# A two-layer decoder step: gemms that add onto PSUM banks seeded by ScalarE, and token sums of the embedding taken four tiles at a time

## The chip, the cores and the metric

One core of a Trainium2 chip runs the whole program. The metric is the device time of one execution in microseconds; the number given for a kernel is the median of its timed runs.

## What is computed

The reference is one inference step of a two-layer decoder on 576 tokens (512 of a prompt, 8 x 8 of samples), width 2048. Cut to what matters here:

```python
y = rmsnorm(x)
proj = y @ w_in                       # 2048 -> 6144: pool input, pool gate, q, k, v, retention gate
o = retention(rope(q), rope(k), v)    # 4 heads of 256
o = head_rmsnorm(o) * silu(gate)
p = pool_mixer(pool_in) * silu(gate)  # 4 groups, windows 2, 4, 8, 16
x2 = x + rmsnorm(concat(p, o) @ w_out)
e = rmsnorm(p_embed @ w_ple)          # per-layer embedding, 256 -> 2048
x = x2 + sigmoid(x2 @ w_gate + b) * e
```

The states of retention and pooling are updated and returned as well.

## The kernel before, in words

Everything is held transposed: 128 features on the partitions, 576 tokens along a row, in two halves of 288 columns (`HN`). A product in float32 precision is made of three float32r matmuls (high x high, high x low, low x high), so weights and activations are split into a high part (ScalarE, L90) and a low part (VectorE, L91).

Each layer has three phases. `in_first` multiplies the first half of the contraction of `w_in` in a Strassen-like scheme (`unit`, L234) and stores 48 tiles in DRAM (`proj_dram`). `in_phase` (L469) takes the second half: `columns(pr)` (L472) loads the stored tile into a buffer `part`, splits two weight blocks and calls `gemm` (L129): 48 matmuls of 288 columns into two PSUM banks `acc`. Then VectorE adds the banks onto the loaded tile (L484), and the consumer works on the tile in SBUF: `rotary` (L491, L492), the gates (L500), v (L579), the pool inputs (L669, L670). There are four `acc` banks, that is two pairs, four `part` buffers and two `g` buffers. Heads 0 to 3 come first (q, k, v, gate: eight tiles each), then pool groups 3, 2, 1, 0 (four tiles each).

`out_phase` multiplies by `w_out`, takes the norm (`rsqrt`, L294), and then makes the embedding: 16 tiles of 12 matmuls each (L767), whose squares (L316, ScalarE) are summed over the partitions by `token_sums` (L290, L292): for each tile four float32 matmuls of a matrix of ones, 144 tokens each, into four groups of 32 columns of TensorE. ScalarE also copies each bank to SBUF (L771). Then come the gates of the layer.

`rsqrt` is a chain that crosses engines: token sums on TensorE, twelve small steps on VectorE (L300 to L306), four matmuls that spread the row (L310, "picks"), two copies by ScalarE (L311). A head ends with it: its output, two tiles `o`, is squared (L635, L636), multiplied by the result (L640) and by the gate (L653), which is the last read of a `g` buffer. Ahead of the squares stand four transposes (L628) with two small adds (L632). The head's keys are transposed (L549) and scaled (L93 on ScalarE, L94 on VectorE). The states of the samples are updated four at a time (L376) between matmuls L359 and L375.

The order of the instructions on each engine is not written by hand: a scheduler sets it from its own estimates when the kernel is built. An engine runs its list strictly in that order, and a tile of a pool waits until the last reader of the buffer's previous tile is done.

Of the kernel before, what the change touches and what calls it, by code (L numbers as in the profile page):

```python
# [10 lines left out]
AF = mybir.ActivationFunctionType  # L11
ALU = mybir.AluOpType
# [21 lines left out]
def half(ap, h):  # L34
    return ap[:, h * HN:(h + 1) * HN]
# [3 lines left out]
def decoder_kernel(ctx: ExitStack, tc: tile.TileContext, a, decay8):  # L39
# [6 lines left out]
    def buf(tag, shape=(P, NT), dt=F32):  # L46
        return sb.tile(list(shape), dt, tag=tag, name=tag, bufs=BUFS.get(tag, 1))
# [75 lines left out]
    def mix_tile():  # L123
        return ps.tile([P, 512], F32, tag="po", name="po", bufs=2)
# [1 line left out]
    def bank(shape):  # L126
        return ps.tile(list(shape), F32, tag="pb", name="pb", bufs=2)

    def gemm(w, xs, new=acc_tile, by_half=False):  # L129
        acc = [new()[:, :HN] for _ in range(2)]  # L130
        n = len(w)
        for hs in ((0,), (1,)) if by_half else ((0, 1),):
            for i, ((wh, wl), (xh, xl)) in enumerate(zip(w, xs)):
                for passno, (u, v) in enumerate(((wh, xh), (wh, xl), (wl, xh))):
                    for h in hs:
                        nc.tensor.matmul(  # L136
                            acc[h], u, v[:, h * HN:(h + 1) * HN],
                            start=(i == 0 and passno == 0), stop=(i == n - 1 and passno == 2),
                        )
        return acc  # L140

# [148 lines left out]
    def token_sums(sums, src, start, stop):  # L290
        for q in range(4):
            nc.tensor.matmul(sums[32 * q:32 * q + 32], ones, src[:, q * QN:(q + 1) * QN], start=start, stop=stop)  # L292

    def rsqrt(out, srcs, n, sums=None):  # L294
        if sums is None:
            sums = mix_tile()[:, :QN]
            for i, src in enumerate(srcs):
                token_sums(sums, src, i == 0, i == len(srcs) - 1)
        v, t, r = (w[:, i * QN:(i + 1) * QN] for w in (tmp(),) for i in range(3))
        nc.vector.tensor_scalar(v, sums, 1.0 / n, EPS, op0=ALU.mult, op1=ALU.add)  # L300
        nc.vector.tensor_scalar(r.bitcast(I32), v.bitcast(I32), 1, None, op0=ALU.logical_shift_right)
        nc.vector.tensor_scalar(r.bitcast(I32), r.bitcast(I32), -1.0, float(0x5F3759DF), op0=ALU.mult, op1=ALU.add)
        for _ in range(3):
            nc.vector.scalar_tensor_tensor(out=t, in0=r, scalar=-0.5, in1=r, op0=ALU.mult, op1=ALU.mult)
            nc.vector.tensor_tensor(out=t, in0=t, in1=v, op=ALU.mult)
            nc.vector.scalar_tensor_tensor(out=r, in0=t, scalar=1.5, in1=r, op0=ALU.add, op1=ALU.mult)  # L306
        for h in range(2):
            rows = mix_tile()[:, :HN]
            for q in (2 * h, 2 * h + 1):
                nc.tensor.matmul(rows[:, (q % 2) * QN:(q % 2 + 1) * QN], pick[:, q], r, start=True, stop=True)  # L310
            nc.scalar.copy(half(out, h), rows)  # L311

    def square(out, src):
        if isinstance(src, list):
            for h in range(2):
                nc.scalar.activation(half(out, h), src[h], AF.Square)  # L316
        else:
            nc.scalar.activation(out, src, AF.Square)

# [11 lines left out]
    def load_tables():  # L331
# [6 lines left out]
        consts["kdec_s"] = load_const("kdec_s", [P, NH, NS])  # L338
        consts["mask_s"] = load_const("mask_s", [P, NH, 64])
        consts["invcnt"] = load_const("invcnt", [P, 4, 16])  # L340

    def after_all(ins, others):
        for other in others:
            tc.add_manual_dep(
                ins.ins, other.ins.name, mybir.DependencyInfo(mybir.DependencyClass.Sync, mybir.DependencyReason.DATA),
                reason="one burst",
            )

    def retention_state(l, h, s0_ring, qrep, kst, vst, po_s):
        for bg in range(2):  # L350
# [118 lines left out]
    def in_phase(l, raws, r2, rB, cos, sin):  # L469
        b_ring, st_ring, rot_ring, s0_ring = Ring(0, 12), Ring(12, 4), Ring(16, 8), Ring(24, 4)  # L470

        def columns(pr):  # L472
            keys = [("in2", p) for p in pairs] + [("out", 0, 0), ("out", 0, 1)]
            i = keys.index(("in2", pr))
            raw = raws.pop(("in2", pr))
            for c in range(2):
                t = buf("part")
                nc.sync.dma_start(out=t, in_=proj_dram[l][2 * pr + c])
                w = split_weights(raw, 8 * c, 8)
                if c == 1:  # L480
                    fetch(l, raws, keys[i + 1:i + 3])
                acc = gemm(w, r2)
                for h in range(2):
                    nc.vector.tensor_tensor(out=half(t, h), in0=acc[h], in1=half(t, h), op=ALU.add)  # L484
                yield t

        def rotary(pr):
            x = [rot_ring.tile() for _ in range(2)]
            u = [buf("d") for _ in range(2)]
            for i, t in enumerate(columns(pr)):  # L490
                nc.vector.tensor_tensor(out=x[i], in0=t, in1=cos, op=ALU.mult)  # L491
                nc.vector.tensor_tensor(out=u[i], in0=t, in1=sin, op=ALU.mult)  # L492
            nc.vector.tensor_tensor(out=x[0], in0=x[0], in1=u[1], op=ALU.subtract)
            nc.vector.tensor_tensor(out=x[1], in0=x[1], in1=u[0], op=ALU.add)
            return x

        def silu_gates(pr):
            for t in columns(pr):
                g = buf("g")
                nc.vector.tensor_tensor(out=g, in0=t, in1=rB, op=ALU.mult)  # L500
                nc.scalar.activation(g, g, AF.Silu)
                yield g

# [56 lines left out]
        def head(h):  # L560
# [14 lines left out]
            kst = sample_rows(sample_part(k, "kdec_s", h), (0, 2))  # L575

            v = [rot_ring.tile() for _ in range(2)]
            for i, t in enumerate(columns(16 + h)):
                nc.vector.tensor_tensor(out=v[i], in0=t, in1=rB, op=ALU.mult)  # L579
            vt = token_major(v)  # L580
            vc = buf("smp", (P, 2, 64))
            for e in range(2):
# [73 lines left out]
        def pool_group(g):  # L656
# [6 lines left out]
            wh, wl = buf("u", (P, 2, DK), F32R), buf("u", (P, 2, DK), F32R)  # L663
            split(wh, wl, wraw)
            xs = []
            for i, t in enumerate(columns(g)):
                e = buf("d", (P, BUF + NP))
                nc.vector.memset(e[:, :BUF], 0.0)
                nc.vector.tensor_tensor(out=e[:, BUF:], in0=t[:, :NP], in1=rB[:, :NP], op=ALU.mult)  # L669
                nc.vector.tensor_tensor(  # L670
                    out=es[:, i, :, BUF:], in0=t[:, NP:].rearrange("p (b s) -> p b s", s=NS),
                    in1=rB[:, NP:].rearrange("p (b s) -> p b s", s=NS), op=ALU.mult,
                )
                nc.scalar.copy(npool[:, i, 0], e[:, NP:NP + BUF])
                nc.scalar.copy(npool[:, i, 1:], es[:, i, :, NS:])
                s, ss, sh = e, es[:, i], 1
                while sh < w:
                    n = tmp()[:, :BUF + NP]
                    m = buf("es", (P, NB, SEG))
                    lo = 2 * sh - 1  # L680
                    nc.gpsimd.tensor_tensor(out=n[:, lo:], in0=s[:, lo:], in1=s[:, sh - 1:BUF + NP - sh], op=ALU.add)
                    nc.gpsimd.tensor_tensor(out=m[:, :, lo:], in0=ss[:, :, lo:], in1=ss[:, :, sh - 1:SEG - sh], op=ALU.add)  # L682
                    s, ss, sh = n, m, 2 * sh
                p = tmp()
                nc.vector.tensor_tensor(out=p[:, :16], in0=s[:, BUF:BUF + 16], in1=consts["invcnt"][:, g], op=ALU.mult)
# [38 lines left out]
    def out_phase(l, raws, ops_out):  # L724
# [30 lines left out]
        for k in range(2):  # L755
# [3 lines left out]
            split(hi, lo, t)  # L759
            pp.append((hi, lo))  # L760
        sums = mix_tile()[:, :QN]
        for c8 in range(2):
            raw = load_weights(a["w_ple"][l, :, c8 * 8:(c8 + 1) * 8].rearrange("p c k n -> p (c k) n"))
            w = split_weights(raw, 0, 16)
            for c in range(8):
                ct = c8 * 8 + c
                acc = gemm(w[2 * c:2 * c + 2], pp)  # L767
                t, sq = buf("part"), buf("u")
                square(sq, acc)
                for i in range(2):  # L770
                    nc.scalar.copy(half(t, i), acc[i])  # L771
                token_sums(sums, sq, ct == 0, ct == KT - 1)
                nc.sync.dma_start(out=ple_dram[l][ct], in_=t)

        def residual(first):
            def xs(k):
# [192 lines left out]
```

## Time and profile before

| | us |
|---|---|
| timed runs, median (lowest to highest of 3) | 2215.37 (2213.88 to 2215.63) |
| the profiled execution | 2217.77 |
| its span on the core | 2216.0 |
| TensorE (PE) busy | 2185.6 (99%) |
| VectorE (DVE) busy | 1733.7 (78%) |
| ScalarE (ACT) busy | 1057.0 (48%) |
| GpSimd (POOL) busy | 174.5 (8%) |

The span is the time from the first to the last instruction on the engines. Busy time counts work; matmuls are pipelined, so a busy TensorE is judged by the distance from one matmul's start to the next one's. "Idle before" in a row is the time for which the engine waited just before, with the work that released it.

### The profile page before, as it was taken

What the parts mean: (1) busy time and instruction counts of PE and PEld (TensorE: products, weight loads), DVE (VectorE), ACT (ScalarE), POOL (GpSimd) and SP (SyncE); (2) the same over time, 40 slices, a digit from 0 to 9 for tenths busy, and PEclk for the clock granted to TensorE, in tenths of its full rate; (3) what the DMA queues carried; (4) which work ended last, traced back from release to release, by engine and by line L of the source; (5) the groups of instructions that cost most, each with busy time, mean ns of one, the idle gap of its engine ahead of it and who ended that gap; (6) DMA issues with size and microseconds to landing.
All of it is one profiled execution on the core that took longest, in us unless ns stands there. A gap on an engine that the chain in (4) does not pass through costs nothing.

```text
span 2216.0 us, 42622 instructions
## 1 busy us (share of the span) xinstructions
PE 2185.6 (99%) x16692; PEld 2143.3 (97%) x16692; DVE 1733.7 (78%) x3146; ACT 1057.0 (48%) x2097; POOL 174.5 (8%) x145
## 2 busy tenths in 40 slices
PE   8999999999999999999999999999999999999998
PEld 8999999999999999899999999999999899998998
DVE  8788766667689998788977886666676899988865
ACT  5465433444334555655545554434443345566532
POOL 2000000000043110000020000000002411100000
PEclk9999999999999999999999999999999999999999
DMA  6455455546443333556644444455555443345554
GB/s 222 149 195 165 155 168 165 169 157 191 154 159 129 133 128 122 196 176 208 216 157 149 169 156 152 160 177 173 164 164 165 155 135 130 106 149 192 176 194 156
DMA packets 137706, 361.99 MB, mean 163 GB/s; under 512 B 14496, under 2 KB 51872, under 8 KB 116640
## 3 DMA queue, kind: packets, MB, share of 16 engines
q1 hardware_dynamic: 137504, 359.26, 49.1%
q8 instruction: 131, 2.15, 0.4%
q14 instruction: 71, 0.58, 0.1%
HBM read 273.17 MB, written 86.04 MB: 162 GB/s over the span
## 4 chain that ended last, share of the span: by engine, by line
PE 87%; DVE 7%; DMA 4%; issue 2%; ACT 0%; SPq 0%; POOL 0%; DVEq 0%; ACTq 0%
PE acc L136 30%; PE acc L118 13%; PE acc L116 13%; PE acc L117 13%; PE acc L226 4%; PE pb L117 3%; PE pb L116 3%; PE pb L118 3%; DMA x<-ple 2%; DVE wl L91 1%; PE po L292 1%; PE po L359 1%; PE pb L375 1%; PE po L136 1%; PE pb L549 1%
## 5 line engine op out<-in xcount | busy, mean ns | idle before, releaser
L136 PE MATMUL acc<-m,wh 128*128 128x288 f32 x3584 | 661.1, 298 | 11.0 <-DVE part L484 11.0
L90 ACT CAST wh<-raw 128x512 fp32r<-128x512 f32 x567 | 350.5, 619 | 506.2 <-PE acc L136 260.7
L117 PE MATMUL acc<-m,wh 128*128 128x288 f32 x1944 | 572.8, 296 | 0.0
L116 PE MATMUL acc<-m,wh 128*128 128x288 f32 x1944 | 571.2, 295 | 0.5 <-ACT m L249 0.5
L118 PE MATMUL acc<-m,wl 128*128 128x288 f32 x1944 | 566.7, 295 | 0.7 <-DVE wl L91 0.7
L136 PEld LDWEIGHTS acc<-m,wh 128*128 128x128 f32 x3584 | 537.9, 190 | 19.1 <-issue 18.0
L91 DVE TENSOR_TENSOR wl<-raw,wh 128x512 fp32r<-128x512 f32 x567 | 407.2, 719 | 134.8 <-ACT wh L90 124.9
L136 PE MATMUL acc<-m,wl 128*128 128x288 f32 x1792 | 399.2, 296 | 0.0
L116 PEld LDWEIGHTS acc<-m,wh 128*128 128x128 f32 x1944 | 364.6, 188 | 1.9 <-ACT m L249 1.0
L117 PEld LDWEIGHTS acc<-m,wh 128*128 128x128 f32 x1944 | 364.9, 188 | 0.0
L118 PEld LDWEIGHTS acc<-m,wl 128*128 128x128 f32 x1944 | 362.4, 188 | 1.4 <-DVE wl L91 1.4
L90 ACT CAST wh<-S 128x512 fp32r<-128x512 f32 x356 | 220.4, 620 | 252.9 <-PE acc L117 139.7
L136 PEld LDWEIGHTS acc<-m,wl 128*128 128x128 f32 x1792 | 294.6, 190 | 1.9 <-issue 1.3
L91 DVE TENSOR_TENSOR wl<-S,wh 128x512 fp32r<-128x512 f32 x356 | 250.5, 705 | 22.0 <-ACT wh L90 20.5
L484 DVE TENSOR_TENSOR part<-acc,part 128x288 f32<-128x288 f32 x192 | 79.3, 449 | 62.4 <-PE acc L136 57.5
L239 POOL TENSOR_TENSOR S<-raw 128x512 f32<-128x512 f32 x45 | 70.3, 1562 | 713.6 <-DVE wl L91 352.6
L239 DVE TENSOR_TENSOR S<-raw 128x512 f32<-128x512 f32 x133 | 93.3, 701 | 8.5 <-DMA raw<-in_w_in 7.0
L682 POOL TENSOR_TENSOR es<-u 128x176 f32<-128x176 f32 x16 | 14.9, 937 | 1055.5 <-DVE u L670 1053.7
L117 PE MATMUL pb<-m,wh 128*128 128x288 f32 x324 | 95.5, 295 | 0.0
L116 PE MATMUL pb<-m,wh 128*128 128x288 f32 x324 | 95.1, 294 | 0.0
L118 PE MATMUL pb<-m,wl 128*128 128x288 f32 x324 | 95.1, 293 | 0.0
L249 ACT COPY d<-acc 128x288 f32<-128x288 f32 x228 | 86.1, 394 | 0.0
(265 smaller groups left out, 3412.1 us busy)
## 6 DMA issues: line engine op xcount, KB each, us to landing
raw<-in_w_in SPq DMA_DIRECT2D x95, 1024.0 KB, 5.3
raw<-in_w_out SPq DMA_DIRECT2D x32, 1024.0 KB, 4.9
raw<-in_w_gate SPq DMA_DIRECT2D x32, 1024.0 KB, 5.3
proj<-d SPq DMA_DIRECT2D x96, 288.0 KB, 2.1
part<-proj SPq DMA_DIRECT2D x96, 288.0 KB, 3.0
m<-in_state_ret SPq DMA_DIRECT2D x64, 256.0 KB, 3.1
out_new_ret_s<-m SPq DMA_DIRECT2D x64, 256.0 KB, 3.4
x<-m SPq DMA_DIRECT2D x48, 288.0 KB, 3.1
```

The costliest lines, as they stand in the source:

```text
L90: nc.scalar.copy(hi, src)
L91: return nc.vector.tensor_tensor(out=lo, in0=src, in1=hi.bitcast(F32), op=ALU.subtract)
L116: nc.tensor.matmul(out, wh, xh, start=start, stop=False, **kw)
L117: nc.tensor.matmul(out, wh, xl, start=False, stop=False, **kw)
L118: nc.tensor.matmul(out, wl, xh, start=False, stop=stop, **kw)
L136: nc.tensor.matmul(acc[h], u, v[:, h * HN:(h + 1) * HN], start=(i == 0 and passno == 0), stop=(i == n - 1 and passno == 2),)
L226: nc.tensor.matmul(acc[h], w[:, j], xs[h][passno == 1], start=(i == 0 and j == 0 and passno == 0), stop=(i == 1 and j == 3 and passno == 2),)
L239: eng.tensor_tensor(out=s, in0=x, in1=y, op=op)
L249: ops["tail_act"] = nc.scalar.copy(dst, src)
L292: nc.tensor.matmul(sums[32 * q:32 * q + 32], ones, src[:, q * QN:(q + 1) * QN], start=start, stop=stop)
L359: mm = nc.tensor.matmul(po_s[32 * r:32 * r + 32, bg], qrep[:, dt, b * 32:b * 32 + 32], s0s[r][:, dt], start=(dt == 0), stop=(dt == 1),)
L484: nc.vector.tensor_tensor(out=half(t, h), in0=acc[h], in1=half(t, h), op=ALU.add)
```

## The change

The loaded tile is no longer added behind the gemm. ScalarE copies it into the two banks first (the seed), the first matmul of each bank then adds instead of overwriting, and `columns` hands out the banks. So the consumers read PSUM, in two halves of 288 columns: rotary reads each bank twice, the gates and v once, the pool inputs in three pieces. In the embedding the squares go into other buffers, and `together` sums four tiles behind each other, with a dependency that makes the first of its matmuls wait for the last square.

```diff
-    def gemm(w, xs, new=acc_tile, by_half=False):
+    def gemm(w, xs, new=acc_tile, by_half=False, seed=None):
         acc = [new()[:, :HN] for _ in range(2)]
+        if seed is not None:
+            for h in range(2):
+                nc.scalar.copy(acc[h], half(seed, h))
...
-                            start=(i == 0 and passno == 0), stop=(i == n - 1 and passno == 2),
+                            start=(seed is None and i == 0 and passno == 0), stop=(i == n - 1 and passno == 2),
+                            skip_group_check=seed is not None,
...
+    def together(sums, srcs, start, stop):
+        for i, src in enumerate(srcs):
+            for q in range(4):
+                mm = nc.tensor.matmul(
+                    sums[32 * q:32 * q + 32], ones, src[:, q * QN:(q + 1) * QN],
+                    start=start and i == 0, stop=stop and i == len(srcs) - 1,
+                )
+                if q == i == 0:
+                    after_all(mm, [last_square[0]])
...
-                acc = gemm(w, r2)
-                for h in range(2):
-                    nc.vector.tensor_tensor(out=half(t, h), in0=acc[h], in1=half(t, h), op=ALU.add)
-                yield t
+                yield gemm(w, r2, seed=t)
+
+        def times(out, acc, row):
+            for h in range(2):
+                nc.vector.tensor_tensor(out=half(out, h), in0=acc[h], in1=half(row, h), op=ALU.mult)
...
-            for i, t in enumerate(columns(pr)):
-                nc.vector.tensor_tensor(out=x[i], in0=t, in1=cos, op=ALU.mult)
-                nc.vector.tensor_tensor(out=u[i], in0=t, in1=sin, op=ALU.mult)
+            for i, acc in enumerate(columns(pr)):
+                times(x[i], acc, cos)
+                times(u[i], acc, sin)
...
-                nc.vector.tensor_tensor(out=g, in0=t, in1=rB, op=ALU.mult)
+                times(g, acc, rB)
...
-                nc.vector.tensor_tensor(out=v[i], in0=t, in1=rB, op=ALU.mult)
+                times(v[i], acc, rB)
...
-                nc.vector.tensor_tensor(out=e[:, BUF:], in0=t[:, :NP], in1=rB[:, :NP], op=ALU.mult)
+                nc.vector.tensor_tensor(out=e[:, BUF:BUF + HN], in0=acc[0], in1=rB[:, :HN], op=ALU.mult)
+                nc.vector.tensor_tensor(out=e[:, BUF + HN:], in0=acc[1][:, :NP - HN], in1=rB[:, HN:NP], op=ALU.mult)
...
-                t, sq = buf("part"), buf("u")
+                t, sq = buf("part"), buf(("tmp", "tmp", "tmp", "tmp", "g", "g", "u", "u")[ct % 8])
...
-                token_sums(sums, sq, ct == 0, ct == KT - 1)
+                squares.append(sq)
+                if len(squares) == 4:
+                    together(sums, squares, ct == 3, ct == KT - 1)
+                    squares = []
```

The scheduler then places everything anew. The lines of the changed kernel stand some numbers further down: its gemm matmul is L141 (before L136), the seed L136, the transposes L647 (L628) and L568 (L549), token sums L298 (L292) and in the embedding L303, picks L326 (L310) and their copies L327 (L311), L659 and L672 are the products with the row and with the gate (L640, L653), and L504 is `times`.

The first place is TensorE at the end of head 0, where the transposes L628 stand. Before, they lie between the matmuls of the next gemm:

```order
L136 MATMUL acc<-m_2419,wh 128x288 x2
L628 MATMUL pb<-c_ident,u 128x128 x4
L136 MATMUL acc<-m_2420,wh 128x288 x2
L136 MATMUL acc<-m_2419,wl 128x288 x2
L136 MATMUL acc<-m_2569,wh 128x288 x2
L136 MATMUL acc<-m_2570,wh 128x288
L549 MATMUL pb<-c_ident,m_3972 128x128
L549 MATMUL pb<-c_ident,m_3973 128x128
```

With the change, in full names, they stand behind each other, and the next gemm comes only after the token sums:

```order
L141 MATMUL acc_4958<-m42_2719,wl_4952 128x288
L647 MATMUL pb_4488<-c_ident_969,u_4486 128x128 x4
L568 MATMUL pb_4532<-c_ident_969,m18_3976 128x128
L568 MATMUL pb_4532<-c_ident_969,m19_3977 128x128
...
L568 MATMUL pb_4543<-c_ident_969,m18_3976 128x128
L568 MATMUL pb_4543<-c_ident_969,m19_3977 128x128
...
L298 MATMUL po_4500<-tmp_4495,ones_61 32x144 x4
L298 MATMUL po_4500<-tmp_4496,ones_61 32x144 x4
L141 MATMUL acc_5050<-m28_1669,wh_5042 128x288
```

No gemm matmul is left among them. acc_5050 takes the bank of acc_4889 (the first tile of the keys); its seed waits for VectorE's last read of that bank, which stands there with the change:

```order
L651 TENSOR_TENSOR m23_4388<-m23_4388,pb_4488 128x64
L94 SCALAR_TENSOR_TENSOR m1_4538<-pb_4532,c_kdec_971,m0_4537 128x256
L504 TENSOR_TENSOR m18_4875<-acc_4889,long_2886 128x288
L504 TENSOR_TENSOR m18_4875<-acc_4890,long_2886 128x288
L504 TENSOR_TENSOR d_4877<-acc_4889,long_2887 128x288
L504 TENSOR_TENSOR d_4877<-acc_4890,long_2887 128x288
```

The reads of acc_4889 come behind L651 and L94, which work on what those transposes give.

The second place is VectorE at the end of head 3, where the pool groups begin, behind the last picks of the heads. Before (o is m22 and m23, part_7858 the loaded tile of the first gemm of pool group 2):

```order
L484 TENSOR_TENSOR part_7858<-acc_7870,part_7858 128x288
L640 TENSOR_TENSOR m22_7038<-m22_7038,tmp_7150 128x576
L640 TENSOR_TENSOR m23_7039<-m23_7039,tmp_7150 128x576
L484 TENSOR_TENSOR part_7858<-acc_7871,part_7858 128x288
L91 TENSOR_TENSOR wl_8155<-raw_7868,wh_8154 128x512
L653 TENSOR_TENSOR m22_7038<-m22_7038,g_7295 128x576
L653 TENSOR_TENSOR m23_7039<-m23_7039,g_7364 128x576
```

And with the change:

```order
L659 TENSOR_TENSOR m22_7084<-m22_7084,tmp_7196 128x576
L659 TENSOR_TENSOR m23_7085<-m23_7085,tmp_7196 128x576
L672 TENSOR_TENSOR m22_7084<-m22_7084,g_7341 128x576
L91 TENSOR_TENSOR m9_8561<-x_8558,m8_8560 128x576
L672 TENSOR_TENSOR m23_7085<-m23_7085,g_7411 128x576
L504 TENSOR_TENSOR g_7679<-acc_7627,long_2859 128x288
L504 TENSOR_TENSOR g_7679<-acc_7628,long_2859 128x288
```

The gate's product now reads the bank itself, and its output g_7679 takes the buffer of g_7341, so the bank acc_7627 stays taken until L672 has read g_7341. The bank is the next gemm's (acc_7831), and TensorE there has, with the change:

```order
L141 MATMUL acc_7714<-m42_2719,wl_7708 128x288
L326 MATMUL po_7219<-tmp_7206,pick_63 128x144 x2
L326 MATMUL po_7223<-tmp_7206,pick_63 128x144 x2
L141 MATMUL acc_7831<-m28_1669,wh_7823 128x288
```

Before, the picks at this place are followed by the last matmuls of a gemm and by the whole of the next; now the first matmul behind them is one that waits for that seed.

The third place is TensorE in the embedding, at the first token sums. Before, seven tiles are summed there, one a little later, and the other eight in two parts each, between the matmuls of the tiles that follow. With the change:

```order
L326 MATMUL po_11249<-tmp_11232,pick_63 128x144 x2
L303 MATMUL po_11265<-tmp_11299,ones_61 32x144 x4
L303 MATMUL po_11265<-tmp_11320,ones_61 32x144 x4
L303 MATMUL po_11265<-tmp_11341,ones_61 32x144 x4
L303 MATMUL po_11265<-tmp_11362,ones_61 32x144 x4
L141 MATMUL acc_11405<-d_11255,wh_11276 128x288
```

Four such groups of sixteen take the place of the eighteen in each layer; the first stands right behind the picks of the norm.

## Rows read from the trace of the kernel before

**Rows 1.** The page: busy time, share of the span and instructions of each engine, and, by engine, the chain of work that ended last.

```profile
PE 2185.6 (99%) x16692; PEld 2143.3 (97%) x16692; DVE 1733.7 (78%) x3146; ACT 1057.0 (48%) x2097; POOL 174.5 (8%) x145
PE 87%; DVE 7%; DMA 4%; issue 2%; ACT 0%; SPq 0%; POOL 0%; DVEq 0%; ACTq 0%
```

**Rows 2.** The chain in order of time: start, length, engine, tile and line; and two rows of TensorE's timeline: start, length, engine, line, operation, out<-in, count, and in brackets the idle time before and what ended it.

```profile
1013.28 86.72 PE acc L136 x665
643.09 0.82 PE L136 MATMUL acc<-m,wh 128*128 128x288 f32 x2 [3.01 <-DVE part L484]
677.01 0.51 PE L136 MATMUL acc<-m,wh 128*128 128x288 f32 x2 [2.48 <-DVE part L484]
```

**Rows 3.** Windows: start and end, length, busy time and count of PE, PEld, DVE, ACT, POOL, then TensorE's granted clock as a share of full speed, the DMA share and GB/s. The first two are of layer 1, the others of layer 2.

```profile
643.00:649.00 6.00, 5.92 (x25) 5.95 (x26) 4.73 (x10) 0.95 (x2) 5.92 (x7) 0.51 0.92 338
649.00:655.00 6.00, 6.00 (x47) 6.00 (x46) 4.10 (x11) 2.83 (x5) 0.33 (x1) 1.00 0.02 5
1737.50:1741.00 3.50, 0.50 (x5) 0.29 (x3) 3.50 (x6) 1.53 (x5) 3.50 (x4) 1.00 0.82 252
1741.00:1747.00 6.00, 6.00 (x34) 6.00 (x35) 4.62 (x10) 0.85 (x2) 5.92 (x7) 0.72 0.91 325
1771.00:1774.00 3.00, 0.52 (x4) 0.31 (x4) 3.00 (x5) 1.15 (x2) 1.73 (x2) 1.00 0.35 100
```

**Rows 4.** Timelines of SyncE's queue and of VectorE, layer 1, ahead of the first wait.

```profile
639.13 0.80 SPq L478 DMA_DIRECT2D part<-proj  x2
642.50 0.81 DVE L484 TENSOR_TENSOR part<-acc,part 128x288 f32<-128x288 f32 x2
```

**Rows 5.** TensorE's timeline in the embedding of layer 1; a float32 matmul of L292 leaves two records.

```profile
891.61 1.92 PE L292 MATMUL po<-u,ones 128*32 128x144 f32 x56
895.24 0.45 PE L292 MATMUL po<-u,ones 128*32 128x144 f32 x8
895.62 0.53 PE L136 MATMUL acc<-d,wh 128*128 128x288 f32 x2
897.19 0.29 PE L136 MATMUL acc<-d,wl 128*128 128x288 f32 x1
897.41 0.44 PE L292 MATMUL po<-u,ones 128*32 128x144 f32 x4
897.78 0.53 PE L136 MATMUL acc<-d,wh 128*128 128x288 f32 x2
898.15 0.29 PE L136 MATMUL acc<-d,wl 128*128 128x288 f32 x1
```

**Rows 6.** Timelines of TensorE, VectorE and ScalarE at the end of head 0 in layer 1, in order of time.

```profile
379.46 0.60 PE L628 MATMUL pb<-c_ident,u 128*128 128x128 f32 x4
379.82 0.51 PE L136 MATMUL acc<-m,wh 128*128 128x288 f32 x2
380.10 0.35 DVE L632 TENSOR_TENSOR m<-m,pb 128x64 f32<-128x64 f32 x2 [0.37 <-PE pb L628]
380.35 0.69 ACT L635 ACTIVATE tmp<-m 128x576 f32<-128x576 f32 x1 [1.35 <-DVE m L632]
380.94 0.67 ACT L636 ACTIVATE tmp<-m 128x576 f32<-128x576 f32 x1
381.52 0.45 ACT L93 ACTIVATE m<-pb,c_kdec 128x256 fp32r<-128x256 f32 x1
383.63 0.70 PE L292 MATMUL po<-tmp,ones 128*32 128x144 f32 x16
```

**Rows 7.** Timelines of VectorE, TensorE, ScalarE and GpSimd at the end of head 3 in layer 1, in order of time.

```profile
604.27 0.31 DVE L304 SCALAR_TENSOR_TENSOR tmp<-tmp 128x144 f32<-128x144 f32 x1
604.61 0.31 DVE L305 TENSOR_TENSOR tmp<-tmp 128x144 f32<-128x144 f32 x1
608.59 1.14 PE L310 MATMUL po<-tmp,pick 128*128 128x144 f32 x8
609.47 0.70 ACT L311 COPY tmp<-po 128x288 f32<-128x288 f32 x2
609.87 3.17 POOL L681 TENSOR_TENSOR tmp<-tmp 128x520 f32<-128x520 f32 x2 [8.65 <-PE po L310]
610.64 3.01 DVE L640 TENSOR_TENSOR m<-m,tmp 128x576 f32<-128x576 f32 x2
614.54 1.41 DVE L653 TENSOR_TENSOR m<-m,g 128x576 f32<-128x576 f32 x2
```

**Rows 8.** VectorE and ScalarE by line and shape: line, engine, operation, names, shapes, count | busy us, mean ns of one | idle time before and what ended it.

```profile
L484 DVE TENSOR_TENSOR part<-acc,part 128x288 f32<-128x288 f32 x192 | 79.3, 449 | 62.4 <-PE acc L136 57.5 <-DMA out_new_ret_s<-m 4.4
L94 DVE SCALAR_TENSOR_TENSOR m<-pb,c_kdec,m 128x256 fp32r<-128x256 f32 x32 | 15.3, 479 | 12.6 <-ACT m L93 12.6
L376 DVE SCALAR_TENSOR_TENSOR m<-m,pb 128x512 f32<-128x512 f32 x64 | 41.8, 682 | 19.3 <-PE po L359 13.8 <-PE pb L375 5.5
L249 ACT COPY d<-acc 128x288 f32<-128x288 f32 x228 | 86.1, 394 | 0.0
```

**Rows 9.** ScalarE's timeline in the embedding of layer 1.

```profile
882.51 0.42 ACT L316 ACTIVATE u<-acc 128x288 f32<-128x288 f32 x1
882.81 0.41 ACT L771 COPY part<-acc 128x288 f32<-128x288 f32 x1
891.15 0.89 ACT L311 COPY long<-po 128x288 f32<-128x288 f32 x2
```

More of the change, by code (lines that the diff above doesn't have):

```diff
@@ L311, in rsqrt, with after_all @@
             nc.scalar.copy(half(out, h), rows)
+    last_square = [None]
+    def after_all(ins, others):
+        for other in others:
+            tc.add_manual_dep(
+                ins.ins, other.ins.name, mybir.DependencyInfo(mybir.DependencyClass.Sync, mybir.DependencyReason.DATA),
+                reason="one burst",
+            )
     def square(out, src):
@@ L315, in square @@
             for h in range(2):
-                nc.scalar.activation(half(out, h), src[h], AF.Square)
+                last_square[0] = nc.scalar.activation(half(out, h), src[h], AF.Square)
         else:
@@ L340, in load_tables @@
         consts["invcnt"] = load_const("invcnt", [P, 4, 16])
[L342 to L347, printed above, removed]
     def retention_state(l, h, s0_ring, qrep, kst, vst, po_s):
@@ L497, in silu_gates @@
         def silu_gates(pr):
-            for t in columns(pr):
+            for acc in columns(pr):
                 g = buf("g")
-                nc.vector.tensor_tensor(out=g, in0=t, in1=rB, op=ALU.mult)
+                times(g, acc, rB)
                 nc.scalar.activation(g, g, AF.Silu)
@@ L577, in head @@
             v = [rot_ring.tile() for _ in range(2)]
-            for i, t in enumerate(columns(16 + h)):
-                nc.vector.tensor_tensor(out=v[i], in0=t, in1=rB, op=ALU.mult)
+            for i, acc in enumerate(columns(16 + h)):
+                times(v[i], acc, rB)
             vt = token_major(v)
@@ L665, in pool_group @@
             xs = []
-            for i, t in enumerate(columns(g)):
+            for i, acc in enumerate(columns(g)):
                 e = buf("d", (P, BUF + NP))
                 nc.vector.memset(e[:, :BUF], 0.0)
-                nc.vector.tensor_tensor(out=e[:, BUF:], in0=t[:, :NP], in1=rB[:, :NP], op=ALU.mult)
+                nc.vector.tensor_tensor(out=e[:, BUF:BUF + HN], in0=acc[0], in1=rB[:, :HN], op=ALU.mult)
+                nc.vector.tensor_tensor(out=e[:, BUF + HN:], in0=acc[1][:, :NP - HN], in1=rB[:, HN:NP], op=ALU.mult)
                 nc.vector.tensor_tensor(
-                    out=es[:, i, :, BUF:], in0=t[:, NP:].rearrange("p (b s) -> p b s", s=NS),
+                    out=es[:, i, :, BUF:], in0=acc[1][:, NP - HN:].rearrange("p (b s) -> p b s", s=NS),
                     in1=rB[:, NP:].rearrange("p (b s) -> p b s", s=NS), op=ALU.mult,
@@ L771, in out_phase @@
                     nc.scalar.copy(half(t, i), acc[i])
-                token_sums(sums, sq, ct == 0, ct == KT - 1)
                 nc.sync.dma_start(out=ple_dram[l][ct], in_=t)
+                squares.append(sq)
+                if len(squares) == 4:
+                    together(sums, squares, ct == 3, ct == KT - 1)
+                    squares = []
         def residual(first):
```

## The prediction, made before the changed kernel was run

> **What bounds the kernel now.** I read the page first: TensorE is busy for 2185.6 of 2216.0 us, and the chain that ended last is TensorE's for 87% [rows 1]. So time is won only where TensorE does useless work, waits or runs slowly, and lost where it gets a new wait. In the chain in order of time a long stretch of gemm takes 86.72 us for 665 matmuls, 0.130 us each [rows 2]; against that pace I looked for stretches of TensorE's timeline that are slower. In the first half of the program the second-half projection has two waits in each layer, where the pool groups are: 3.01 and 2.48 us, both ended by VectorE's add L484 [rows 2]. Behind the first the granted clock falls to 0.51 of full (about 1.2 GHz): 25 matmuls in 6 us, then 47 at the full clock [rows 3]. In layer 2 it is 0.72, 34 matmuls [rows 3]. Last I read the embedding, where each visit of the ones matmul L292 breaks the pace [rows 5].
>
> **The old waits: about -15 us.** Ahead of the first wait the load of the `part` tile is issued only at 639.13, because its buffer was in use by VectorE's late readers, and the add stands at 642.50 behind VectorE's backlog [rows 4]. With the change the seed frees the `part` buffer as soon as ScalarE has copied it, so loads run ahead, and no add is left. The price of the old waits: in layer 1 3.0 + 2.5 us, and for the clock 6 us less 25 x 0.130, 2.7 us; in layer 2 two waits like them (0.50 us of work in 3.5 us, 0.52 in 3.0 [rows 3]) and 6 less 34 x 0.130, 1.6 us. That is 8.2 + 7.1 = 15 us. I find no late load at these places in the new order, so I take all of it; the other end is 12, if the clock alone stays low.
>
> **The bursts: about -11 us.** Between 897.19 and 898.15 three gemm matmuls and one visit of half a tile take 0.96 us, so the visit costs 0.96 - 0.39 = 0.57 [rows 5]. A visit of one tile holds TensorE 0.38 (895.24 to 895.62), one of seven tiles 1.85 (891.61 to 893.46) [rows 5]: 0.245 a tile more, and 0.33 for going in and out. Before, a layer has 16 half tiles (9.1), one tile (0.58) and one of seven (2.05), 11.7 us; after, four of four tiles (1.31 each), 5.2. The gain is 6.5 a layer. Against it: the first group stands right behind the picks and must wait for a square that ScalarE makes after the two copies of the picks' result. Before, L292 starts at 891.61 [rows 5], 0.46 behind the start of these copies at 891.15 [rows 9]; now 0.89 for the copies and 0.30 and 0.42 for the last two squares [rows 9] come ahead of it, 1.6, or 1.15 more a layer. So 5.4 a layer, 11 in all. Ends: 13 if the squares come earlier, 5 if ScalarE becomes the limit. A tile costs it two squares and two copies at a distance of 0.30 (882.51 to 882.81 [rows 9]), 1.2 us, and a share of casts, against 1.9 for TensorE; so I take neither end.
>
> **Work that is hidden.** 192 adds of 449 ns [rows 8], 79 us of VectorE, go; reading in halves gives some of it back (rotary reads four times 0.45 in place of twice 0.75). 192 copies of about 0.394 (the row of the same shape between PSUM and SBUF [rows 8]), 76 us, come to ScalarE, which is busy for less than half the span [rows 1]. Neither is on the path by itself: in most gemms over 6 us of matmuls lie between the reads that the seed waits for and the seed's use. The path is hit where that distance is gone.
>
> **Head ends: about +12 us.** Before, the transposes at 379.46 are followed by gemm matmuls at 379.82, and TensorE is covered until the token sums at 383.63 [rows 6]. In the new order twelve transposes and eight ones matmuls stand there, and the next gemm's seed waits for reads that stand behind L651 and L94. I lay the durations of these rows along it, from the first transpose. VectorE's small adds start at 0.64 (380.10), the squares can start at 0.9 (380.35), and each takes 0.59 until the next can start (380.35 to 380.94) [rows 6]. ScalarE first scales a block of keys (0.45 [rows 6]) and ends it at 1.5, VectorE's L94 takes 0.48 [rows 8] to 2.0, three reads of 0.45 at a distance of about 0.41 end at 3.2, and the seed ends at 3.65. TensorE has 12 transposes (0.09 each by the same rows) and two one-tile sums, 1.9 us. So it idles 1.8; in heads 1 and 2 its transposes also wait for the state updates, 0.3 more. Three heads in two layers: 12 us. Ends: 5, if VectorE is ahead, and 17, if it stands back by one more L376 (0.68 [rows 8]).
>
> The Trainium skill says, in "Perfetto Trace Analysis", section "Optimizing Tensor Performance", that independent matmul groups should rotate through different PSUM banks, so that the evacuation of one overlaps the next one's matmuls. The two pairs do rotate, so by that rule alone this term would be nothing and the forecast below 12 us lower. The rows speak against it at this place, since evacuation itself waits for work that TensorE has just done.
>
> **Start of the pool groups: about +24 us.** Here TensorE in the new order runs out three times in each layer.
> - Four state updates at 0.68 [rows 8] alternate with their matmuls with no gemm between; a cast ahead of them counted, the chain is 4.1 us against 2.1 of TensorE's: 2.0.
> - The small steps of the row's chain come at a distance of 0.34 (604.27 to 604.61 [rows 7]); twelve, with five splits between them, need 7.3 us until the picks can start. TensorE has 46 matmuls, 5.9: 1.4.
> - Then the chain that I think costs most. It stands in the trace of before, with a gemm beside it: picks at 608.59, copies at 609.47, L640 at 610.64, which takes 3.01 for two instructions while GpSimd works on the pool (609.87 for 3.17 us), L653 from 614.54 to 615.95 [rows 7]. That is 7.4 us. Without the two adds L484 between (0.37 each) it is 6.6; the gate's read and the seed add 0.45 and 0.39; the picks themselves are 0.8. TensorE waits 6.6 us, since its next matmul needs that seed.
> - After such a wait the clock falls as it did behind 3.01 us: 2.2, the mean of 2.7 and 1.6.
>
> Sum 12.2 a layer, 24. Ends: 12 (the last two without contention and without a fall) and 30.
>
> **One more: +2 us.** Some seventy matmuls on, a seed waits behind two L703 that wait for TensorE; about 1 a layer, from 0 to 2.
>
> **Sum.** -15 - 11 + 12 + 24 + 2 = +12 on the profiled 2217.77: 2229.8. That execution stood 2.4 us above the median, so I forecast **2227.4 us**, slower by 0.5%.
>
> **The rivals.**
> - *Faster.* VectorE loses 79 us of adds, and it was the late one before [rows 4]. If its queue therefore stands earlier than the rows of before say, it is ahead of TensorE at the head ends and the state updates, and those waits close. Only the chain behind the picks stays, because TensorE's own picks start it: 2 x (6.6 + 2.2) = 18. This decides when the reads at a head's end come 1.8 us sooner than I have them. -15 - 11 + 18 = -8: 2207. Against it: at the head ends the queue's place doesn't matter, since the reads wait for transposes and ScalarE's copy.
> - *The clock falls at head ends too.* The waits are some 2 us, in pieces. At 2.48 the trace shows no fall, at 3.01 it does [rows 2, 3]. If six falls of 2.7 come, +16: 2243. The Trainium skill has such a case in "TensorE: Matmul & The Clock Gate", section "A second HAM failure mode: psum-queue depth-cycling": short idle times between groups that cycle through PSUM banks made the clock go back and forth. The trace of before has two isolated waits only and can't show it.
> - *ScalarE limits the embedding* and its gain falls to nothing: 2238.
> - *Even.* The new waits are real but a third shorter, 25 in place of 38, because a step of the walks overlaps the one before it: -1 on the sum, 2214, no change. A seed that overwrote nothing or did not take effect would alter values and not the time.
>
> **How the numbers follow.** The forecast 0.55, the faster case 0.17, the clock 0.1, ScalarE 0.06, a third shorter 0.12. The low ends of all terms give about -15 - 13 + 5 + 12 = -11, 2204, the high ends -12 - 5 + 17 + 30 + 4 = +34, 2249; the ends won't all fall together, and I take **2207 to 2241**, which takes in most of the faster case's neighbourhood and half of the clock's. About 0.2% (4.4 us) is what a measurement of this kernel can tell from no change. Faster by more than that: the faster case and a little of the shorter waits, 0.2. Within: what lies between, 0.15. Slower: 0.65. The forecast's own range is 2218 to 2238.
>
> **What would show it.** In the new profile: no wait by a late add in the pool groups; at each end of heads 0 to 2 TensorE idle by about 2 us, ended by ScalarE's seed L136; behind the last picks of head 3 a wait of 6 to 7 us, ended by the seed, and a clock near half for some 6 us behind it; four visits of L303 in each embedding, the first behind a wait of nearly 2 us on a square. I am wrong if TensorE passes the head ends without a wait, if the wait behind the picks is under 3 us, or if the embedding gets no shorter than 8 us in both layers.

## The result and the profile after

The changed kernel takes **2246.58 us** (median of 4 runs, 2243.57 to 2247.55) beside 2214.74 for the kernel before: a ratio of 1.0141, 95% interval 1.0124 to 1.0159. The forecast was 2227.4 with a range of 2207 to 2241, so the direction was right and the size was not: +12 us forecast, +31.8 between the medians and +29.8 between the two profiled executions, which the account below splits up.

The page of the changed kernel: busy time by engine, and the chain that ended last, by engine.

```profile
PE 2183.3 (97%) x16692; PEld 2144.8 (96%) x16692; DVE 1672.9 (74%) x3082; ACT 1124.3 (50%) x2289; POOL 162.2 (7%) x145
PE 87%; DMA 5%; DVE 5%; ACT 2%; issue 1%; SPq 0%; POOL 0%; DVEq 0%; ACTq 0%
```

Beside [rows 1], VectorE has lost 61 us and ScalarE has gained 67, where 79 less what the reads in halves give back and 76 were costed; TensorE is still the bound. It does the same work in a span that is 30 us longer, so the loss is time in which it waits or runs at a low clock. Its waits, by what ended them: line, releaser, us in total, times, longest.

```profile
PE acc L141 <- ACT acc L136: 19.0, 10, 6.4
...
PE po L377 <- issue: 4.5, 2, 4.2
PE po L377 <- DMA m<-in_state_ret: 3.3, 3, 2.3
PE pb L568 <- DVE m L651: 3.0, 6, 0.7
PE acc L141 <- ACT part L792: 2.7, 3, 1.0
PE po L377 <- DMA u<-in_w_pool: 2.6, 1, 2.6
PE po L303 <- ACT tmp L341: 2.2, 2, 1.1
```

The row left out is alike in both kernels (L232, 6.1 us, for a cast of weights). The waits by L484 [rows 2] are gone, and the forecast seed wait is the longest. Nothing in the forecast answers to the three rows of L377, 10.4 us in all. TensorE's timeline at the places the forecast spoke of and at two it didn't: the end of head 0, the state tiles of head 1 and of head 3, the picks of head 3, the embedding.

```profile
375.31 0.60 PE L647 MATMUL pb<-c_ident,u 128*128 128x128 f32 x4
375.75 0.60 PE L568 MATMUL pb<-c_ident,m 128*128 128x128 f32 x4
377.04 0.63 PE L568 MATMUL pb<-c_ident,m 128*128 128x128 f32 x4 [0.69 <-DVE m L651]
377.60 0.96 PE L298 MATMUL po<-tmp,ones 128*32 128x144 f32 x16
379.27 0.54 PE L141 MATMUL acc<-m,wh 128*128 128x288 f32 x2 [0.71 <-ACT acc L136]
...
446.05 1.07 PE L377 MATMUL po<-m,u 128*32 128x256 f32 x16 [2.27 <-DMA m<-in_state_ret]
...
595.63 1.07 PE L377 MATMUL po<-m,u 128*32 128x256 f32 x16 [2.64 <-DMA u<-in_w_pool]
...
612.22 1.25 PE L326 MATMUL po<-tmp,pick 128*128 128x144 f32 x8 [0.72 <-DVE tmp L322]
619.87 0.85 PE L141 MATMUL acc<-m,wh 128*128 128x288 f32 x2 [6.40 <-ACT acc L136]
...
626.15 0.43 PE L141 MATMUL po<-u 128*128 128x288 f32 x2
...
896.55 0.75 PE L298 MATMUL po<-tmp,ones 128*32 128x144 f32 x16
898.26 0.53 PE L141 MATMUL acc<-d,wh 128*128 128x288 f32 x2 [0.95 <-ACT part L792]
...
905.38 1.19 PE L303 MATMUL po<-tmp,ones 128*32 128x144 f32 x32 [1.10 <-ACT tmp L341]
```

Where [rows 6] has gemm matmuls between transposes and sums, there are two gaps here; where [rows 7] has a gemm behind the picks, 6.40 us are empty.

**The account.** I took each distance between two matmuls' starts against what that pair takes when nothing waits (0.130 us for two of a gemm), and set the excess of after against that of before. "Visits" are the ones matmuls' own time, and "clock" is what matmuls lose at a low granted clock. The parts add up to +29.8:

| place | forecast | measured |
|---|---|---|
| old waits, with their low clock | -15 | -17.1 (waits -11.6, clock -5.5) |
| bursts: visits | -13 | -12.8 |
| bursts: waits behind them | +2 | +8.2 |
| head ends | +12 | +12.5 |
| state tiles loaded late (L377), with their low clock | - | +11.2 |
| start of the pool groups, with its low clock | +24 | +24.6 |
| the seed some seventy matmuls on | +2 | +2.7 |
| the rest | - | +0.5 |

**The late loads.** SyncE's queue ahead of the wait at 446.05, and the same loads at the end of head 3 in both layers:

```profile
431.66 1.10 SPq L372 DMA_DIRECT2D m<-in_state_ret  x2
432.86 0.42 SPq L102 DMA_DIRECT2D raw<-in_w_in  x1
433.37 0.90 SPq L395 DMA_DIRECT2D out_new_ret_s<-m  x2
...
442.40 1.05 SPq L372 DMA_DIRECT2D m<-in_state_ret  x2
...
591.46 1.07 SPq L372 DMA_DIRECT2D m<-in_state_ret  x2
...
1704.29 1.06 SPq L372 DMA_DIRECT2D m<-in_state_ret  x2
```

A head's eight state tiles go through four buffers: a load L372 waits until the store L395 of the buffer's last tenant has landed. The two stores at 433.37 stand behind a 1 MB load of weights, and the two loads are issued 9 us after them. In its own list SyncE waits 88.6 us for that, against 67.0 before, and TensorE pays for the end of it. The two rows of L377 that name `issue` and a load of pool weights are of the same kind: at the end of head 3 the last state loads are issued at 591.46 and 1704.29, 7 and 9 us behind the stores that they wait for, and land by 595.49 and 1708.09; L377 starts at 595.63 and 1708.18.

**The clock.** Windows of after: start and end, length, busy time and count of PE, PEld, DVE, ACT, POOL, the granted clock, the DMA share and GB/s.

```profile
447.00:451.00 4.00, 4.00 (x22) 3.96 (x19) 1.98 (x3) 1.62 (x3) 0.00 (x0) 0.57 0.63 164
456.00:461.00 5.00, 4.30 (x41) 3.98 (x38) 5.00 (x14) 2.69 (x8) 0.00 (x0) 1.00 0.62 185
595.60:600.00 4.40, 3.56 (x26) 2.40 (x27) 3.11 (x7) 1.39 (x4) 0.24 (x1) 0.75 0.49 165
620.00:627.00 7.00, 6.97 (x34) 6.74 (x34) 6.97 (x10) 4.02 (x8) 6.76 (x7) 0.64 0.27 85
1708.00:1712.00 4.00, 3.09 (x20) 1.68 (x20) 1.61 (x3) 1.10 (x2) 0.00 (x0) 0.50 0.26 97
```

Behind the wait of 2.27 us the granted clock is 0.57 of full, near the lower level (1.2 GHz), behind the one of 6.40 it is 0.64, and behind the late loads of head 3 it is 0.75 and 0.50 (595.60 and 1708). At a head's end (456 to 461) it stays full. The state updates that I counted to the start of the pool groups run in those two stretches, so a part of that term belongs to the late loads.

### The profile page after: what moved, and what is told of

Its sections match the earlier page's. It is cut to its first block, busy times and chain, and to the rows that moved or that the text cites. A ratio compares the mean times of both kernels' runs of the same rounds, so it can differ in the third digit from the quotient of the medians.

```text
span 2245.8 us, 42762 instructions
## 1 busy us (share of the span) xinstructions
PE 2183.3 (97%) x16692; PEld 2144.8 (96%) x16692; DVE 1672.9 (74%) x3082; ACT 1124.3 (50%) x2289; POOL 162.2 (7%) x145
## 4 chain that ended last, share of the span: by engine, by line
PE 87%; DMA 5%; DVE 5%; ACT 2%; issue 1%; SPq 0%; POOL 0%; DVEq 0%; ACTq 0%
PE acc L141 32%; PE acc L117 13%; PE acc L116 13%; PE acc L118 13%; PE acc L232 4%; PE pb L117 3%; PE pb L116 3%; PE pb L118 3%; DMA x<-ple 2%; PE po L141 1%; DMA out_new_ret_s<-m 1%; PE po L377 1%; PE pb L393 1%; PE po L326 1%; PE pb L568 1%
## 5 line engine op out<-in xcount | busy, mean ns | idle before, releaser
L141 PE MATMUL acc<-m,wh 128*128 128x288 f32 x3584 | 660.0, 298 | 19.0 <-ACT acc L136 19.0
L90 ACT CAST wh<-raw 128x512 fp32r<-128x512 f32 x567 | 350.8, 620 | 518.0 <-PE acc L141 250.8
L118 PE MATMUL acc<-m,wl 128*128 128x288 f32 x1944 | 566.6, 295 | 0.0
L141 PEld LDWEIGHTS acc<-m,wh 128*128 128x128 f32 x3584 | 540.7, 190 | 24.8 <-ACT acc L136 21.6
L141 PE MATMUL acc<-m,wl 128*128 128x288 f32 x1792 | 409.7, 297 | 0.0
L90 ACT CAST wh<-S 128x512 fp32r<-128x512 f32 x356 | 220.9, 620 | 240.1 <-PE acc L117 142.0
L141 PEld LDWEIGHTS acc<-m,wl 128*128 128x128 f32 x1792 | 297.9, 190 | 3.2 <-issue 2.9
L136 ACT COPY acc<-part 128x288 f32<-128x288 f32 x192 | 76.1, 400 | 31.4 <-DVE d L504 18.0
```

The source lines that it names most:

```text
L90: nc.scalar.copy(hi, src)
L118: nc.tensor.matmul(out, wl, xh, start=False, stop=stop, **kw)
L136: nc.scalar.copy(acc[h], half(seed, h))
L141: nc.tensor.matmul(acc[h], u, v[:, h * HN:(h + 1) * HN], start=(seed is None and i == 0 and passno == 0), stop=(i == n - 1 and passno == 2 ...
```

## The experiments

Ratios are to the kernel before on the same chip, with 95% intervals. "The change" is the changed kernel, and "the kernel of 2" the one that experiment 2 makes of it.

**1. Each half alone.** Without seeds:

```
-                yield gemm(w, r2, seed=t)
+                acc = gemm(w, r2)
+                for h in range(2):
+                    nc.vector.tensor_tensor(out=half(t, h), in0=acc[h], in1=half(t, h), op=ALU.add)
+                yield t
```

> No seeds: the projection's second half as before, only the embedding's squares summed four tiles at a time. Theory A (the visits of the ones matmul are priced right, 0.57 each for half a tile, 1.3 for four tiles, but ScalarE's copies free the banks late in that stage): the gross gain of 12.8 us is halved by waits on ScalarE, so 2208 to 2212 beside 2214.7 for the kernel before. Rival B (the late copies came only because the seeds had moved the order): the whole gain, 2202. Rival C (the embedding is ScalarE's and nothing is won): 2214 or more.

Measured: 2210.25, 0.9974 [0.9963, 0.9986]. The sums alone gain 5.8 us, as theory A has it; the old waits stand (3.23 and 2.48 in layer 1). The first two waits of the embedding, 0.95 and 1.10 us, stand too, so they don't come from the seeds.

With seeds, and with the embedding of before:

```
+                token_sums(sums, sq, ct == 0, ct == KT - 1)
-                squares.append(sq)
-                if len(squares) == 4:
-                    together(sums, squares, ct == 3, ct == KT - 1)
-                    squares = []
```

> Seeds as in the change, the embedding as before. Theory A: all of the loss lies in the projection's second half, and the embedding's small gain is missing: 2249 to 2251. Rival D (a part of the loss came with the bursts, by waits on ScalarE): 2240 to 2245.

Measured: 2252.79, 1.0161 [1.0142, 1.0180]. That is a little above theory A, and rival D falls: the whole loss comes with the seeds.

**2. The state tiles.** Three of a head's eight get a buffer that is idle there, so that fewer loads wait for a store:

```
-                s0 = s0_ring.tile((P, 2, DK))
+                s0 = buf("S", (P, 2, DK)) if bg == 1 and r < 3 else s0_ring.tile((P, 2, DK))
```

> The change, and three of the eight state tiles of a head take buffers of tag S, which lie idle in this phase, in place of the ring of four; so their loads need not wait for the store of the tile before. Theory E (the waits at head ends and ahead of L377 both come from the late state tiles: the first by the order that the scheduler makes of it, the second directly): 12.5 + 9.7 + some 2 of low clock go, 2221 to 2224; in the trace no wait over 0.5 us at a head's end. Rival F (K's reads of the banks make the head ends wait whatever the states do): only the L377 waits go, 2234 to 2236. Rival G (seeding itself is slow, by ScalarE's copies and reads from PSUM in halves): above 2240.

Measured: **2209.82**, 0.9974 [0.9964, 0.9985], which is 37 us less than the change and 11 below what theory E gave. TensorE's waits in it:

```profile
PE acc L141 <- ACT acc L136: 15.0, 4, 6.7
PE acc L232 <- ACT wh L90: 6.3, 1, 6.3
PE po L303 <- ACT tmp L341: 2.2, 2, 1.1
```

L377 and the transposes L568 are gone from the list, the wait behind the picks is not. SyncE waits 45.6 us for the states' stores, where it was 88.6 in the change. Its timeline at the end of head 0:

```profile
368.83 0.60 PE L647 MATMUL pb<-c_ident,u 128*128 128x128 f32 x4
369.18 0.38 PE L141 MATMUL acc<-m,wh 128*128 128x288 f32 x1
369.40 0.60 PE L568 MATMUL pb<-c_ident,m 128*128 128x128 f32 x4
369.76 0.51 PE L141 MATMUL acc<-m,wh 128*128 128x288 f32 x2
```

The gemm stands between the transposes again, as in [rows 6]. I had taken the bare head ends for something the seeds do by themselves. With the state buffers the scheduler doesn't build them, though the seeds are all there. Of the 39 us between the two profiled executions (37 between the medians), head ends are some 12.5, the waits at L377 9.7, the state updates, the wait ahead of the picks and the low clock behind the late loads some 12, and later waits in the embedding and at the layers' ends some 4. From the picks to the end of the pool groups the two traces lose nearly the same: the seed some seventy matmuls on still waits, 0.87 us beside 1.19. The three buffers and the new order that the scheduler made for them came in one edit, so how much each is worth isn't shown; the waits at L377 alone are 9.7.

The same edit in the kernel before:

> The kernel before (no seeds, no bursts of four) with the three state tiles in buffers of tag S. Theory E' (it is the seeds that make the states late, so without seeds there is little to win): the waits ahead of L359, 1.6 us in all, go, 2212 to 2215. Rival J (the extra buffers are worth the same with or without seeds, so the gain of the third experiment says nothing of the seeds): 2190 or less, since that experiment won 37 us.

Measured: 2210.19, 0.9965 [0.9951, 0.9978], between the two: some 8 us below the kernel before. The loads themselves can hardly be that gain, since TensorE waited only 0.9 us ahead of L359 and SyncE's waits for the stores rise (67.0 to 86.7 us); what falls is the wait by L484, from 11.0 us to 2.4. So here the gain seems to come with the order that the scheduler makes, which no run separates. With the state tiles out of the way, change and before are level (0.9974 and 0.9965, intervals that overlap).

**3. The wait behind the picks.** The gate's product holds a bank because its output waits for a buffer `g`. So it gets more of them, in three runs: `"g": 2` becomes 3 in the change, 4 in the kernel of 2, and 4 in the change.

> The change with three g buffers instead of two. Theory H (the wait of 6.6 us behind the last picks is made by the gate's output that takes the buffer which L672 still reads): the bank is read a gemm earlier, the wait goes in both layers and with it the low clock behind it: 13 + 3 us less than the change, 2229 to 2233, if what now comes next (a seed one gemm later) has its 6 us of matmuls ahead of it. Rival I (the chain only moves by a gemm, since VectorE's list is the same): 2240 to 2246.

> The third experiment's kernel with four g buffers. Theory H' (the wait behind the picks is made by the two gates' outputs, so it takes two buffers more and not one): both waits of 6.8 and 6.9 us go and the low clock behind them, 2.9 in all, while the products of the pool (po<-u) come up to 2 us late: 2209.8 - 16.6 + 2 = 2193 to 2197. Rival I (the chain moves on by another gemm): 2205 or more.

> The change with four g buffers and nothing else: the states stay late. Theory H' with E: the picks' wait goes (13.2 + 3), head ends and L377 stay: 2230 to 2234. Rival K (the late states and the picks' wait are one chain, so that one does not go without the other): 2242 or more.

Measured, in that order: 2244.19, 1.0130 [1.0115, 1.0145]; 2212.88, 0.9977 [0.9967, 0.9987]; 2249.38, 1.0150 [1.0132, 1.0167]. None gains, so theories H and H' fall and the times are the rivals'. With three the same wait (6.66 us as a distance) stands one gemm later. With four no seed waits there, but the products of the pool do, for ScalarE's split of the pooled row (L90): 5.4 us in the kernel of 2, 4.9 and 4.4 in the change. Then the gates with the add of before, so that no gate holds a bank for long, in the kernel of 2:

```
-            for acc in columns(pr):
-                times(g, acc, rB)
+            for t in columns(pr, False):
+                nc.vector.tensor_tensor(out=g, in0=t, in1=rB, op=ALU.mult)
```

> The change with the three state buffers, but with the gates' second half added by VectorE through a tile in SBUF as before; q, k, v and the pool's inputs stay on seeded banks. Theory N (the wait of 6.8 us behind the picks comes from the gates' banks, which VectorE's state updates hold): it goes in both layers, 13 us less than the change with the state buffers, less some 3 to 6 us of smaller waits for the pool's products: 2199 to 2203 us. Rival I (the wait belongs to VectorE's queue behind the picks and moves to the pool's products whatever the gates do): 2207 to 2211 with a wait of over 4 us for an operand of the pool within 20 us behind the picks in layer 1.

Measured: 2216.55, 0.9999 [0.9991, 1.0008]. Theory N falls: the wait moves to the pool's products in both layers, as rival I has it, and the time is above both. TensorE's timeline in this kernel:

```profile
599.71 1.14 PE L326 MATMUL po<-tmp,pick 128*128 128x144 f32 x8
614.93 0.85 PE L141 MATMUL po<-u 128*128 128x288 f32 x2 [5.56 <-ACT u L90]
617.62 1.33 PE L141 MATMUL po<-u 128*128 128x288 f32 x4 [1.84 <-DVE u L91]
```

And in the kernel before, behind the picks of [rows 7]:

```profile
621.76 0.53 PE L136 MATMUL po<-u 128*128 128x288 f32 x2 [0.32 <-ACT u L90]
```

From the picks to the first product of the pool it is 13.2 us before (608.59 to 621.76), 13.9 in the change, 13.8 in the kernel of 2 and 15.2 here, with a chain on VectorE, GpSimd and ScalarE in between. What differs most is TensorE's work beside it. Before, 88 gemm matmuls stand there, 11.4 us at 0.130. In the change there are 29 (3.8 us), in the kernel of 2 30, here 64. **In the change the cover has gone, and the price is about what it was.** In this kernel both count: 3.1 us less cover than before and 2.0 us more chain, for a wait that is 5.2 us longer. With four buffers in the kernel of 2 the first product comes after 10.7 us and 62 matmuls, and the wait of 5.4 stands at a later product, 17.8 us behind the picks. VectorE's queue in the change shows the chain itself:

```profile
613.94 2.00 DVE L659 TENSOR_TENSOR m<-m,tmp 128x576 f32<-128x576 f32 x2 [1.16 <-ACT tmp L327]
615.86 0.75 DVE L672 TENSOR_TENSOR m<-m,g 128x576 f32<-128x576 f32 x1
616.53 1.81 DVE L91 TENSOR_TENSOR m<-x,m 128x576 fp32r<-128x576 f32 x1
618.27 0.75 DVE L672 TENSOR_TENSOR m<-m,g 128x576 f32<-128x576 f32 x1
618.94 0.81 DVE L504 TENSOR_TENSOR g<-acc,long 128x288 f32<-128x288 f32 x2
```

Why the scheduler places fewer matmuls there isn't shown, and an order with the seeds and with all 88 was not tried. So that the cover decides is argued from the counts.

**4. The embedding.** ScalarE's timeline in the change, at the first two groups of sums:

```profile
895.54 1.26 ACT L343 ACTIVATE tmp<-m 128x576 f32<-128x576 f32 x2
896.71 0.60 ACT L90 CAST wh<-raw 128x512 fp32r<-128x512 f32 x1
897.22 0.70 ACT L341 ACTIVATE tmp<-acc 128x288 f32<-128x288 f32 x2
897.81 0.70 ACT L792 COPY part<-acc 128x288 f32<-128x288 f32 x2
...
903.83 0.89 ACT L327 COPY long<-po 128x288 f32<-128x288 f32 x2
904.61 0.72 ACT L341 ACTIVATE tmp<-acc 128x288 f32<-128x288 f32 x2
```

At 898.26 TensorE waits for the copies at 897.81, and at 905.38 for the squares at 904.61 behind the copies of the picks' result. Two tries to relieve ScalarE. One of each tile's two copies on VectorE, in the kernel with state buffers and four `g`:

```
-                for i in range(2):
-                    nc.scalar.copy(half(t, i), acc[i])
+                nc.vector.tensor_copy(half(t, 0), acc[0])
+                nc.scalar.copy(half(t, 1), acc[1])
```

> The sixth experiment's kernel, with one of the two copies of each embedding tile made by VectorE in place of ScalarE. Theory C' (the waits of 1.16 and 1.32 us at the start of each embedding and those at its end are ScalarE's queue): 2 to 4 us less than the sixth. Rival L (they wait for the squares and the picks and not for the copies): the same within 1 us.

Measured: 2228.01, 1.0048 [1.0033, 1.0063], 15 us worse than without the edit, and both theories fall. The gemm now waits 8.1 us for copies on ScalarE and 3.9 for those on VectorE, where they stand behind the residual's products of 0.7 us each (L805, L808). Second, the two squares at 895.54 on VectorE, in the kernel with the old gates:

```
-            square(t, mo[KT - 2 + i])
+            nc.vector.tensor_tensor(out=t, in0=mo[KT - 2 + i], in1=mo[KT - 2 + i], op=ALU.mult)
```

> The kernel of the run above with the squares of the output projection's last two tiles (two instructions of 0.7 us a layer) on VectorE instead of ScalarE. Theory O (the first wait of the embedding, 0.95 to 1.2 us for ScalarE's copies behind those squares, is ScalarE's backlog): that wait falls below 0.3 us in both layers, the other one behind the picks' copies stays, and the time falls by 1 to 2 us. Rival P (the wait is for the copies themselves, whatever stands ahead of them): the wait stays over 0.8 us and the time within 0.5 us.

Measured: 2217.48, 1.0002 [0.9993, 1.0011]; the wait falls from 0.95 to 0.69 us, and the time not at all. Theory O gets 0.26 us of the 0.65 or more that it gave; the copies of the tile itself keep the rest, which is nearer to rival P. The cast behind the squares starts at 882.90 with them on ScalarE and at 882.86 without, since it waits for the gemm, and the tile's own squares and copies follow it as they did.

**5. What the two good parts give.** The sums in groups of four with the state buffers, no seeds:

> The kernel before with the four-tile sums and with three of a head's eight state tiles in idle buffers; no seeds. Theory A (what the sums gave alone, 5.8 us, and what the state buffers gave alone, about 5 to 8 us, lie in different stages and add): 2202 to 2206 us beside about 2216. Rival M (the state buffers and the sums work on one slack, so that only one of the two counts): 2208 to 2211.

Measured: **2204.2**, 0.9949 [0.9934, 0.9964], the best of all. Both gains add, as theory A has it. The sums gain 5.8 us alone, and by the ratios 4.4 beside the seeds (1.0161 to 1.0141) and 3.5 beside the state buffers (0.9965 to 0.9949), with intervals that overlap. Behind the picks stand 87 gemm matmuls:

```profile
603.57 1.15 PE L326 MATMUL po<-tmp,pick 128*128 128x144 f32 x8
617.21 0.53 PE L141 MATMUL po<-u 128*128 128x288 f32 x2 [0.91 <-ACT u L90]
```

The first of the old waits in layer 1 is down to 1.18 us in it and the second is gone, and in the kernel before with the state buffers as well; so a good part of what the seeds were to bring is had without them.

## Why the prediction was wrong in size

- **The step that failed** is one that the sum did not have: DMAs that the change's new order moves. I followed TensorE, VectorE and ScalarE through the three places and never SyncE's queue, where a state load waits for a store in the same ring. The forecast's one sentence on late loads in the new order is about the `part` tiles of the pool groups. The late state loads cost 9.7 us of waits and 1.5 of clock, 11.2 of the 17.8 us that the sum lacks; the waits behind the bursts, 8.2 against 2, are 6.2 more.
- **Bursts, -11**: the price of a visit was right (12.8 saved, 13 worked out), the waits were not. I had one new wait a layer, for the squares, at 1.15 us more than before. There are two (0.95 and 1.10 us idle, 1.2 and 1.3 as distances), and in layer 1 later ones of about 1 us, two where a gemm waits for ScalarE's copies and one at the layer's end for VectorE (L825), 8.2 in all. So by its own sign (an embedding shorter by 8 us in both layers, which I read as the sum of the two) this term was wrong: 4.6 are left. My reason, 1.2 us of ScalarE a tile against 1.9 of TensorE, is a mean, and ScalarE has just then the norm's squares, casts and the picks' copies.
- **Old waits, -15**: -17.1. In layer 2 of the kernel before the clock had fallen behind the second wait of 2.48 us too. So the forecast's reading that the trace shows no fall at 2.48 holds for layer 1 alone.
- **Head ends, +12**: 12.5, at the places and for the reads that were named, though about half of the wait at head 0 stands ahead of the transposes L568 (0.69 at 377.04) and not ahead of the seed (0.71 at 379.27). That they are the seeds' own was only argued, and experiment 2 shows it false: the same seeds have no such place once the state tiles are loaded early.
- **Pool start, +24**: 24.6. The wait behind the picks was put at 6.6 and is 6.66 as a distance in both layers; the clock follows. Its reason was half right. The bank held by a gate is how it shows, and taking that away only moves it (experiment 3); in all the orders that wait there, fewer matmuls stand between. The state updates came out near the forecast, 4.5 against 4, in part by luck: 1.8 of it are waits for VectorE's updates (L394), as forecast, and the rest is the low clock behind the late loads.
- The rival in which the clock falls at the head ends did not come: between 375 and 531 it is low only behind L377's wait of 2.27 us. The rival in which ScalarE limits the embedding was half true, and it and the late loads together made the size.

## What to carry to other kernels

When a change makes a scheduler place the program anew, walk the queue that issues DMAs as closely as the engines, above all loads that wait for a store in a small ring: three more buffers there, with the order that the scheduler then made, were worth 37 us. And for each chain that is hidden, count the matmuls that cover it before and after, since here a chain of about the same length that had lost two thirds of its cover was a wait, and taking one resource of it away only moved that wait.

## What the runs showed of the hardware

- The granted clock fell behind waits of 2.27 and 2.64 us in the change (0.57 and 0.75), and in the kernel before it stayed at 1.00 behind the wait of 2.48 us in layer 1 [rows 2] and fell to 0.50 behind the one of 2.48 us in layer 2, which ends at 1773.86. So the length of a wait alone did not decide it. The windows before:

```profile
677.00:683.00 6.00, 5.99 (x45) 6.00 (x46) 5.80 (x15) 2.39 (x4) 0.93 (x1) 1.00 0.59 180
1776.00:1778.00 2.00, 2.00 (x10) 2.00 (x10) 2.00 (x6) 0.00 (x0) 0.00 (x0) 0.50 0.87 273
```

- The two products of 576 columns behind the picks took 3.01 us beside 3.17 us of GpSimd's adds [rows 7], 2.00 in the change beside one add of 1.05 (613.61), and 1.42 in the kernel of experiment 5, where GpSimd's add ended before them.
- A visit of four tiles by the ones matmul cost 1.3 us beside the gemm, as worked out from visits of half a tile, one and seven.
